# Moving the GpSimd sums and splits of the second MLP layer to VectorE in a one-core decoder trunk

## The chip, the core and the metric

The kernel runs on one core of one Trainium2 chip, in one launch. A core has five engines that each work through a queue of their own in order and wait for one another by semaphores: TensorE (PE in the profile; its weight loads are listed as PEld), VectorE (DVE), ScalarE (ACT), GpSimd (POOL) and SyncE (SP), which here only starts transfers. Transfers run on 16 shared DMA engines. The metric is device time in microseconds (us) of the whole launch; lower is better. Three runs of the kernel before took 2007.76, 2008.43 and 2013.69 us, median 2008.43.

## The reference

With DEPTH = 1 only the first layer runs: a Conformer convolution module and a squared-ReLU MLP, each behind an RMS norm and added to the residual.

```
h = rms_norm(x, mix_norm)                         # x: 1 x 2048 x 1024, float32
a, g = split(h @ w_in + b_in)                     # 1024 -> 2 x 1024
h = depthwise_causal_conv31(a * sigmoid(g)) + conv_b
x = x + silu(layer_norm(h)) @ w_out + b_out
n = rms_norm(x, mlp_norm)
x = x + square(relu(n @ w1)) @ w2                 # 1024 -> 4096 -> 1024
```

The last line's `@ w2` is the "second layer" here: for each token, 4096 hidden values to 1024 outputs.

## The kernel before, in words

Everything is kept transposed: 128 features on the partitions, 512 tokens (T) along the free axis, so the 2048 tokens are four token blocks. Each float32 operand is split in two parts (a rounded part and the rest), and a product is three matmuls: high by high, high by low, low by high.

Token blocks 0 and 1 go through the MLP directly. Token blocks 2 and 3, the last two, go through both MLP layers by a seven-product scheme for 2 x 2 blocks (Strassen's idea in Winograd's form): of the weight blocks A11, A12, A21, A22 it forms S1 = A21 + A22, S2 = S1 - A11, S3 = A11 - A21, S4 = A12 - S2, and it multiplies seven pairs in place of eight.

The second layer of these two token blocks is the last stage, from about 1607 us to the end. It runs over eight groups g of hidden features and two halves o of the outputs, 16 steps in all; here they are called step 0 to step 15, step = 2g + o. A step does this:

- SyncE loads two raw weight tiles (`raw_wq`, L590, tile `rawq`, 512 KB each): a1 holds A11 and A12, a2 holds A21 and A22. There are four such buffers, so a step's two loads go into the buffers of the step two before, once that step has done with them.
- `blocks` (L837) forms the sums: S1 at L842, S2 at L843, S3 in place of A21 at L847, S4 in place of A12 at L849. Then `w_split` (L582 to L586) splits each of the seven blocks: ScalarE casts the high part (L584), and the engine that is handed over subtracts it for the low part (L585). The tile is `wq`; six of them exist, so a split waits until TensorE has done the product six before.
- TensorE does the products in the order P1 (A11), P2 (A12), P6 (S2), P5 (S1), P7 (S3), P3 (S4), P4 (A22), each as two tiles of six matmuls (L609), 84 matmuls in a step. P1, P6, P7 and P4 add up in the same PSUM tiles `px`; after P7 VectorE adds `px` and `p` (L872, "px add" below), and P4 can't write `px` before that read is over.
- The four output pairs leave as adding DMAs (L883, `accum_op=ALU.add`, 512 KB each) that GpSimd issues.
- Every two steps the 14 hidden tiles of a later group are loaded (L598, tile `ld`) and split by ScalarE and VectorE (L92, L93), most of them during an odd step, the last during step 11.

In step 0 VectorE forms S1 and S2, in steps 1 to 15 GpSimd does; the split of A22 is GpSimd's in all 16. A scheduler orders each engine's instructions by the order of the program and its own forecast of when data arrive, so an instruction of a later step can stand in a queue ahead of one of an earlier step.

Of the kernel before, what the change touches and what calls it, by code (L numbers as in the profile page):

```python
# [59 lines left out]
def conformer_mlp(ctx: ExitStack, tc, xT, w_in, w_out, w1, w2, vecs, conv_w, outT):  # L60
    nc = tc.nc
# [371 lines left out]
    def mlp_down(g, blocks, hid, x2, eng=nc.vector):  # L433
        for m in range(KD):
            if m % 2 == 0:
                w = load_w2(g, m, eng)
            for i, b in enumerate(blocks):
                ps = bank()
                mm(ps, lambda k, a: w(m % 2, k, a), hid[i])
                nc.vector.tensor_add(x2[i][m], x2[i][m], ps)  # L440
                if g == NG - 1:
                    nc.sync.dma_start(outT[m * P : (m + 1) * P, b * T : (b + 1) * T], x2[i][m])

    def mlp(g, blocks, x2, xs, eng=nc.vector):
        mlp_down(g, blocks, mlp_up(g, xs, eng), x2, eng)
# [112 lines left out]
    def mid_tile(name):  # L558
        return mid.tile([P, T], F32, name=name, tag="m", bufs=6)
# [22 lines left out]
    def w_split(src, eng):  # L582
        hl = wts.tile([P, 2, T], F32R, name="wq", tag="wq", bufs=N_WQ)
        nc.scalar.copy(hl[:, 0, :], src)  # L584
        eng.tensor_sub(hl[:, 1, :], src, hl[:, 0, :].bitcast(F32))  # L585
        return hl  # L586

    def raw_wq(src):
        t = top.tile([P, 2 * T], F32, name="rawq", tag="rawq", bufs=4)
        nc.sync.dma_start(t if src.shape == t.shape else t.rearrange("p (s q c) -> p s q c", s=2, q=2), src)  # L590
        return t
# [245 lines left out]
    def blocks(g, o):  # L837
        a1, a2 = [raw_wq(w2[g, o][:, 2 * i : 2 * i + 2]) for i in range(2)]
        a11, a12, a21, a22 = a1[:, :T], a1[:, T:], a2[:, :T], a2[:, T:]
        s1, s2 = mid_tile("s1"), mid_tile("s2")  # L840
        eng = nc.gpsimd if g or o else nc.vector
        eng.tensor_add(s1, a21, a22)  # L842
        eng.tensor_sub(s2, s1, a11)  # L843
        out = {"A11": w_split(a11, nc.vector), "A12": w_split(a12, nc.vector)}
        out["S2"] = w_split(s2, nc.vector)
        out["S1"] = w_split(s1, nc.vector)
        nc.vector.tensor_sub(a21, a11, a21)  # L847
        out["S3"] = w_split(a21, nc.vector)
        nc.vector.tensor_sub(a12, a12, s2)  # L849
        out["S4"] = w_split(a12, nc.vector)  # L850
        out["A22"] = w_split(a22, nc.gpsimd)
        return out

    def both(tiles, name, hs, w, first=True):
# [97 lines left out]
```

## Time and profile before

| what | value |
|---|---|
| median of three runs | 2008.43 us |
| the profiled execution, its own time | 2008.22 us |
| its span, first to last instruction | 2006.5 us |
| TensorE busy | 1894.8 us, 94% of the span |
| VectorE busy | 1605.4 us, 80% |
| ScalarE busy | 826.8 us, 41% |
| GpSimd busy | 649.6 us, 32% |
| mean granted TensorE clock | 0.981 of full |

The shares are means over stages that differ. In the last fifth of the span, where the change lies, TensorE is busy some eight tenths of the time and its granted clock dips, while VectorE is at five to six tenths. So the page has to be read by stage: which engine waits, for whom, and what ended that wait last.

### The profile page before, as it was taken

The page shows a single profiled execution, that of the slowest core. Times are in us where ns is not written, and L with a number is a line of the kernel's source. Part 1 is how long each engine was busy: PE and PEld are TensorE (multiplying, and loading weights), DVE is VectorE, ACT ScalarE, POOL GpSimd, SP SyncE. Part 2 cuts the span into 40 slices and gives each one's busy share as a digit, 9 for nine tenths or more (in the row PEclk, how much of TensorE's full clock was granted, in tenths as well). Part 3 has the DMA queues.
Part 4 walks back from the last instruction along what each step waited for, and adds up shares of the span by engine and source line. Part 5 has one row for each costly group of instructions (what it writes and reads, how often), then busy time and mean ns, then how long its engine had stood idle before and what let it go on. Part 6 is the DMA issues. An engine that isn't in the chain of part 4 may idle for free.

```text
span 2006.5 us, 23614 instructions
## 1 busy us (share of the span) xinstructions
PE 1894.8 (94%) x8192; PEld 1546.0 (77%) x8192; DVE 1605.4 (80%) x2318; ACT 826.8 (41%) x1336; POOL 649.6 (32%) x433
## 2 busy tenths in 40 slices
PE   7999999999899999999999989999999978888887
PEld 6888888888778778788888768878888766666675
DVE  7999999999999999799999735695886675565553
ACT  5323225243353333433231524464545655454542
POOL 2256322644445530000000004304665343333333
PEclk9999999999999999999999999999999998999999
DMA  5123222422224333642121458656765687787876
GB/s 197 64 85 116 91 76 73 144 97 98 85 82 144 106 111 111 219 144 98 62 69 65 161 194 292 233 189 225 239 222 187 212 226 199 195 205 199 201 147 182
DMA packets 141623, 303.15 MB, mean 151 GB/s; under 512 B 13632, under 2 KB 40384, under 8 KB 141504
## 3 DMA queue, kind: packets, MB, share of 16 engines
q1 hardware_dynamic: 133440, 272.28, 40.6%
q0 software_dynamic: 8064, 29.36, 8.3%
q8 instruction: 64, 1.05, 0.2%
q14 instruction: 55, 0.45, 0.1%
HBM read 210.12 MB, written 91.47 MB: 150 GB/s over the span
## 4 chain that ended last, share of the span: by engine, by line
PE 37%; issue 9%; DVE 5%; DMA 5%; POOL 3%; ACT 2%; SPq 0%; DVEq 0%; POOLq 0%; ACTq 0%
PE ps L163 16%; PE px L609 12%; PE pz L609 4%; PE py L609 3%; PE px L163 2%; DVE wq L585 1%; POOL x L883 1%; DVE act L93 1%; DMA s<-conv 1%; DMA rawq<-in_w_out 1%; POOL s L842 1%; DMA ld<-hT 1%; DVE p L872 1%; DMA c<-x 1%; ACT act L92 1%
## 5 line engine op out<-in xcount | busy, mean ns | idle before, releaser
L163 PE MATMUL ps<-act,w 128*128 128x512 f32 x2880 | 665.5, 391 | 10.9 <-ACT w L92 8.5
L163 PEld LDWEIGHTS ps<-act,w 128*128 128x128 f32 x2880 | 541.3, 188 | 126.9 <-ACT w L92 8.5
L163 PE MATMUL ps<-hid,w 128*128 128x512 f32 x1920 | 446.2, 392 | 6.1 <-DVE hid L93 5.9
L609 PE MATMUL px<-act,wq 128*128 128x512 f32 x1536 | 386.1, 405 | 61.3 <-DVE p L872 47.7
L163 PEld LDWEIGHTS ps<-hid,w 128*128 128x128 f32 x1920 | 360.5, 189 | 86.8 <-DVE hid L93 8.6
L609 PEld LDWEIGHTS px<-act,wq 128*128 128x128 f32 x1536 | 299.5, 196 | 134.6 <-DVE p L872 53.6
L352 DVE SCALAR_TENSOR_TENSOR cacc<-hc,cw,cacc 128x512 f32<-128x512 f32 x464 | 324.7, 749 | 1.4
L352 DVE SCALAR_TENSOR_TENSOR cacc<-h,cw,cacc 128x512 f32<-128x512 f32 x464 | 316.7, 746 | 0.0
L93 POOL TENSOR_TENSOR w<-raw,w 128x1024 fp32r<-128x1024 f32 x90 | 217.0, 2411 | 288.5 <-ACT w L92 282.7
L92 ACT CAST w<-raw 128x1024 fp32r<-128x1024 f32 (+1 forms) x150 | 155.1, 1035 | 291.0 <-PE ps L163 286.5
L609 PE MATMUL pz<-act,wq 128*128 128x512 f32 x768 | 186.4, 392 | 4.5 <-ACT p L828 2.6
L585 DVE TENSOR_TENSOR wq<-rawq,wq 128x512 fp32r<-128x512 f32 x128 | 123.2, 969 | 68.5 <-ACT wq L584 68.5
L609 PEld LDWEIGHTS pz<-act,wq 128*128 128x128 f32 x768 | 144.9, 189 | 35.5 <-ACT p L828 3.0
L584 ACT CAST wq<-rawq 128x512 fp32r<-128x512 f32 x192 | 117.9, 620 | 124.1 <-DMA rawq<-in_w_out 38.7
L585 POOL TENSOR_TENSOR wq<-rawq,wq 128x512 fp32r<-128x512 f32 x64 | 92.4, 1444 | 236.2 <-ACT wq L584 164.9
L440 DVE TENSOR_TENSOR h<-h,ps 128x512 f32<-128x512 f32 x128 | 86.9, 683 | 31.4 <-PE ps L163 29.7
L427 ACT ACTIVATE relu<-ps 128x512 f32<-128x512 f32 x64 | 38.2, 597 | 161.4 <-PE ps L163 161.3
L93 DVE TENSOR_TENSOR act<-ld,act 128x512 fp32r<-128x512 f32 x112 | 82.6, 756 | 22.7 <-ACT act L92 22.1
L609 PE MATMUL py<-act,wq 128*128 128x512 f32 x384 | 94.6, 395 | 2.9 <-DVE cc L697 2.9
L163 PE MATMUL px<-act,wq 128*128 128x512 f32 x384 | 89.9, 395 | 7.7 <-ACT act L92 7.1
L215 POOL TENSOR_TENSOR acc<-acc,hc 128x512 f32<-128x512 f32 x12 | 14.0, 1163 | 252.1 <-DVE hc L352 201.9
L92 ACT CAST act<-ld 128x512 fp32r<-128x512 f32 x112 | 69.0, 620 | 61.3 <-DMA ld<-hB 27.8
(135 smaller groups left out, 1861.4 us busy)
## 6 DMA issues: line engine op xcount, KB each, us to landing
raw<-in_w SPq DMA_DIRECT2D x104, 512.0 KB, 3.6
rawq<-in_w SPq DMA_DIRECT2D x76, 512.0 KB, 4.9
xt<-in_xT SPq DMA_DIRECT2D x64, 256.0 KB, 3.7
ld<-hT SPq DMA_DIRECT2D x64, 256.0 KB, 5.5
raw<-in_w_in SPq DMA_DIRECT2D x30, 512.0 KB, 3.2
x<-p POOLq DMA_DIRECT2D x28, 512.0 KB, 7.6
hB<-cc SPq DMA_DIRECT2D x48, 256.0 KB, 2.8
ld<-hB SPq DMA_DIRECT2D x48, 256.0 KB, 6.2
```

The lines of the kernel that those rows point to most:

```text
L92: nc.scalar.copy(hl[:, 0, :], src)
L93: eng.tensor_sub(hl[:, 1, :], src, hl[:, 0, :].bitcast(F32))
L163: nc.tensor.matmul(ps, lhsT=w(k, a), rhs=x[:, b, :], start=k == 0 and i == 0, stop=k == len(xs) - 1 and i == 2,)
L352: nc.vector.scalar_tensor_tensor(out, h[:, k : k + T], cw[:, j, k : k + 1], acc, ALU.mult, ALU.add)
L427: nc.scalar.activation(r, ps, AF.Relu)
L440: nc.vector.tensor_add(x2[i][m], x2[i][m], ps)
L584: nc.scalar.copy(hl[:, 0, :], src)
L585: eng.tensor_sub(hl[:, 1, :], src, hl[:, 0, :].bitcast(F32))
L609: nc.tensor.matmul(ps, lhsT=hl[:, a, off + k * P : off + (k + 1) * P], rhs=x[:, b, :], start=first and k == 0 and i == 0, stop=k == n - 1 ...
L842: eng.tensor_add(s1, a21, a22)
L872: nc.vector.tensor_add(c[:, i, :], ps, t[:, i, :])
L883: nc.gpsimd.dma_start(at, c, accum_op=ALU.add)
```

## The change

GpSimd loses three instructions per step: S1, S2 and the low part of A22. VectorE gets them. In the program's text the two sums also move behind the splits of A11 and A12, and since L841 goes, every later line number is smaller by one in the kernel after (L872 becomes L871, L883 becomes L882).

```
-        eng = nc.gpsimd if g or o else nc.vector
-        eng.tensor_add(s1, a21, a22)
-        eng.tensor_sub(s2, s1, a11)
         out = {"A11": w_split(a11, nc.vector), "A12": w_split(a12, nc.vector)}
+        nc.vector.tensor_add(s1, a21, a22)
+        nc.vector.tensor_sub(s2, s1, a11)
         out["S2"] = w_split(s2, nc.vector)
         out["S1"] = w_split(s1, nc.vector)
         nc.vector.tensor_sub(a21, a11, a21)
         out["S3"] = w_split(a21, nc.vector)
         nc.vector.tensor_sub(a12, a12, s2)
         out["S4"] = w_split(a12, nc.vector)
-        out["A22"] = w_split(a22, nc.gpsimd)
+        out["A22"] = w_split(a22, nc.vector)
```

The queues of TensorE keep their order. VectorE's order changes in the second layer only. First place: VectorE in step 4 (even), from the adds of P2 (`p1_13801`) to the px adds (`p5_13846`). `rawq_13965` is a1 of step 5, `rawq_14108` and `rawq_14110` are a1 and a2 of step 6, `s2_13970` is S2 of step 5. Before:

```order
L872 TENSOR_TENSOR p1_13801<-py_13786,p1_13801 128x512
L585 TENSOR_TENSOR wq_13973<-rawq_13965,wq_13973 128x512
L847 TENSOR_TENSOR rawq_14110<-rawq_14108,rawq_14110 128x512
L585 TENSOR_TENSOR wq_13976<-rawq_13965,wq_13976 128x512
L849 TENSOR_TENSOR rawq_13965<-rawq_13965,s2_13970 128x512
L585 TENSOR_TENSOR wq_13979<-s2_13970,wq_13979 128x512
L872 TENSOR_TENSOR p5_13846<-px_13783,p5_13846 128x512
```

The same place in the kernel after, from the split of A22 of step 4 (`wq_13780`) on:

```order
L585 TENSOR_TENSOR wq_13780<-rawq_13754,wq_13780 128x512
L871 TENSOR_TENSOR p1_13801<-py_13785,p1_13801 128x512
L871 TENSOR_TENSOR p1_13801<-py_13786,p1_13801 128x512
L585 TENSOR_TENSOR wq_13971<-rawq_13965,wq_13971 128x512
L842 TENSOR_TENSOR s1_14112<-rawq_14110 128x512
L843 TENSOR_TENSOR s2_14113<-s1_14112,rawq_14108 128x512
L846 TENSOR_TENSOR rawq_14110<-rawq_14108,rawq_14110 128x512
L585 TENSOR_TENSOR wq_13974<-rawq_13965,wq_13974 128x512
L848 TENSOR_TENSOR rawq_13965<-rawq_13965,s2_13970 128x512
L585 TENSOR_TENSOR wq_13979<-s2_13970,wq_13979 128x512
L871 TENSOR_TENSOR p5_13846<-px_13783,p5_13846 128x512
```

In both, an instruction on step 6's weights stands ahead of step 4's px add: before it is L847, which waits for GpSimd's S1 of step 6; after it is S1 itself, then S2, then the same subtraction.

Second place: VectorE in step 3 (odd), from the split of A11 of step 4 to the px add (`p5_13703`), with the splits of hidden tiles (L93) between. `rawq_13967` is a2 of step 5. Before:

```order
L585 TENSOR_TENSOR wq_13760<-rawq_13752,wq_13760 128x512
L93 TENSOR_TENSOR act_13917<-ld_13915,act_13917 128x512
L93 TENSOR_TENSOR act_13922<-ld_13920,act_13922 128x512
L847 TENSOR_TENSOR rawq_13967<-rawq_13965,rawq_13967 128x512
L585 TENSOR_TENSOR wq_13763<-rawq_13752,wq_13763 128x512
L93 TENSOR_TENSOR act_13927<-ld_13925,act_13927 128x512
L849 TENSOR_TENSOR rawq_13752<-rawq_13752,s2_13757 128x512
L93 TENSOR_TENSOR act_13932<-ld_13930,act_13932 128x512
L585 TENSOR_TENSOR wq_13766<-s2_13757,wq_13766 128x512
L872 TENSOR_TENSOR p5_13703<-px_13640,p5_13703 128x512
```

After:

```order
L93 TENSOR_TENSOR act_13917<-ld_13915,act_13917 128x512
L842 TENSOR_TENSOR s1_13969<-rawq_13967 128x512
L93 TENSOR_TENSOR act_13922<-ld_13920,act_13922 128x512
L843 TENSOR_TENSOR s2_13970<-s1_13969,rawq_13965 128x512
L585 TENSOR_TENSOR wq_13761<-rawq_13752,wq_13761 128x512
L93 TENSOR_TENSOR act_13927<-ld_13925,act_13927 128x512
L848 TENSOR_TENSOR rawq_13752<-rawq_13752,s2_13757 128x512
L93 TENSOR_TENSOR act_13932<-ld_13930,act_13932 128x512
L585 TENSOR_TENSOR wq_13766<-s2_13757,wq_13766 128x512
L871 TENSOR_TENSOR p5_13703<-px_13640,p5_13703 128x512
```

S1 and S2 of step 5 stand where L847 stood; that subtraction (now L846) comes 20 instructions later, behind the px adds.

Third place: GpSimd in steps 3 and 4. Before, the adding DMAs stand between sums and split:

```order
L842 TENSOR_TENSOR s1_13969<-rawq_13967 128x512
L843 TENSOR_TENSOR s2_13970<-s1_13969,rawq_13965 128x512
L883 DMA x2_1_3_9335<-p5_13703 128x1024
L883 DMA x2_1_2_9334<-u2_13688 128x1024
L883 DMA x2_0_3_9331<-c_13748 128x1024
L585 TENSOR_TENSOR wq_13780<-rawq_13754,wq_13780 128x512
```

After, from the DMA ahead of these on:

```order
L882 DMA x2_0_2_9330<-p1_13658 128x1024
L882 DMA x2_1_3_9335<-p5_13703 128x1024
L882 DMA x2_1_2_9334<-u2_13688 128x1024
L882 DMA x2_0_3_9331<-c_13748 128x1024
L882 DMA x2_0_0_9328<-p1_13801 128x1024
```

Up to step 13, only the issuing of the adding DMAs is left on GpSimd in this layer.

## Rows read from the trace of the kernel before

**Rows 1.** Two stretches: start:end us, busy PE, PEld, DVE, ACT, POOL, clock, DMA, GB/s

```profile
1500.00:1600.00 100.00, 98.11 (x429) 80.77 (x428) 68.05 (x81) 60.00 (x105) 49.85 (x35) 0.99 0.56 194
1750.00:1800.00 50.00, 41.83 (x176) 33.55 (x175) 29.40 (x44) 26.25 (x47) 17.14 (x16) 0.93 0.82 205
```

**Rows 2.** Who waited for whom, 1645 to 2007: us in total, times, longest

```profile
DVE rawq L847 <- POOL s L842: 92.8, 13, 11.7
POOL s L842 <- DMA rawq<-in_w: 80.6, 13, 9.9
...
PE px L609 <- DVE p L872: 47.4, 13, 7.2
```

**Rows 3.** Timeline of TensorE, P4 with the next P1: start, us, [idle before]

```profile
1654.65 7.35 PE L609 MATMUL px<-act,wq 128*128 128x512 f32 x24 [2.96 <-DVE p L872]
...
1681.88 7.88 PE L609 MATMUL px<-act,wq 128*128 128x512 f32 x24 [6.29 <-DVE p L872]
...
1704.60 5.74 PE L609 MATMUL px<-act,wq 128*128 128x512 f32 x24 [1.24 <-DVE p L872]
...
1782.30 7.16 PE L609 MATMUL px<-act,wq 128*128 128x512 f32 x24 [6.29 <-DVE p L872]
...
1881.97 8.46 PE L609 MATMUL px<-act,wq 128*128 128x512 f32 x24 [6.02 <-DVE p L872]
...
1904.19 5.73 PE L609 MATMUL px<-act,wq 128*128 128x512 f32 x24 [0.16 <-DVE p L872]
...
1926.89 5.75 PE L609 MATMUL px<-act,wq 128*128 128x512 f32 x24 [3.37 <-DVE p L872]
```

**Rows 4.** Timeline of step 2 (even), landing of step 4's weights to px add

```profile
1676.25 1.25 POOL L842 TENSOR_TENSOR s<-rawq 128x512 f32<-128x512 f32 x1 [9.56 <-DMA rawq<-in_w]
1677.54 0.69 DVE L847 TENSOR_TENSOR rawq<-rawq 128x512 f32<-128x512 f32 x1 [11.38 <-POOL s L842]
1677.58 1.77 POOL L843 TENSOR_TENSOR s<-s,rawq 128x512 f32<-128x512 f32 x1
1678.15 1.75 DVE L585 TENSOR_TENSOR wq<-rawq,wq 128x512 fp32r<-128x512 f32 x1
1679.93 0.69 DVE L849 TENSOR_TENSOR rawq<-rawq,s 128x512 f32<-128x512 f32 x1
1680.54 0.69 DVE L585 TENSOR_TENSOR wq<-s,wq 128x512 fp32r<-128x512 f32 x1
1681.14 1.28 DVE L872 TENSOR_TENSOR p<-px,p 128x512 f32<-128x512 f32 x2
```

**Rows 5.** Timeline of step 3 (odd), landing of step 5's weights to px add

```profile
1697.82 1.29 POOL L842 TENSOR_TENSOR s<-rawq 128x512 f32<-128x512 f32 x1 [2.86 <-DMA rawq<-in_w]
...
1699.75 1.78 DVE L585 TENSOR_TENSOR wq<-rawq,wq 128x512 fp32r<-128x512 f32 x1
...
1703.87 0.67 DVE L872 TENSOR_TENSOR p<-px,p 128x512 f32<-128x512 f32 x1
```

**Rows 6.** Timeline of step 2: A22's split, and step 4's two weight loads

```profile
1661.83 3.94 SPq L590 DMA_DIRECT2D rawq<-in_w  x2
...
1663.40 0.62 ACT L584 CAST wq<-rawq 128x512 fp32r<-128x512 f32 x1
...
1664.11 1.30 POOL L585 TENSOR_TENSOR wq<-rawq,wq 128x512 fp32r<-128x512 f32 x1 [3.08 <-ACT wq L584]
```

**Rows 7.** Stretches of 3 us in steps 2 and 3, columns as in rows 1

```profile
1664.00:1667.00 3.00, 3.00 (x15) 2.49 (x14) 1.68 (x3) 1.72 (x4) 2.18 (x2) 1.00 1.05 263
...
1676.00:1679.00 3.00, 0.00 (x0) 0.00 (x0) 1.46 (x2) 0.25 (x1) 2.67 (x2) 1.00 0.01 4
...
1682.00:1685.00 3.00, 3.00 (x7) 2.37 (x8) 2.82 (x5) 0.15 (x1) 1.35 (x2) 0.50 0.31 29
...
1700.00:1703.00 3.00, 3.00 (x15) 2.44 (x13) 3.00 (x4) 1.16 (x3) 0.98 (x1) 1.00 0.71 210
```

**Rows 8.** Instructions on `rawq` from 1600 us: ns min/median/max, first and last start

```profile
L585 DVE TENSOR_TENSOR wq<-rawq,wq x62: 672/684/1790, 1613.1 to 1974.4; 128x512 fp32r<-128x512 f32 x62
```

## The prediction, made before the changed kernel ran

> **What bounds the kernel now.** I read the page by slices first, then the last stage by stretches. In a stretch before the second layer TensorE is busy 98 of 100 us, in one inside it 42 of 50, with the clock at 0.93 and VectorE at 29 of 50 [rows 1]. So TensorE waits there, and not because VectorE is full.
>
> The waits of that stage say for whom. The largest wait of TensorE is for the px add: 47.4 us in 13 waits. VectorE itself waits 92.8 us in 13 times at L847 for GpSimd's S1, and GpSimd waits 80.6 us in 13 times for the raw weights [rows 2]. These are one chain: a weight tile of a later step lands, GpSimd adds S1, VectorE goes on with what stands ahead of the px add in its queue, then the px add lets P4 start.
>
> The timeline of step 2 shows it link by link [rows 4]. The weights land at 1676.25; S1 takes 1.25; L847 starts at 1677.54; the split of A12 takes 1.75 beside GpSimd's S2; L849 and the split of S2 follow; the px add starts at 1681.14. That is 4.89 us from landing to px add, and P4 starts when the first of its two halves is done, at 1681.88, after 6.29 us of idle TensorE [rows 3]. In step 3 the same chain, with hidden splits between, takes from 1697.82 to 1703.87, 6.05 us [rows 5], and P4 waits 1.24 us. After the long wait 24 matmuls take 7.88 us where they take 5.74 after a short one [rows 3]; the granted clock in that stretch is 0.50, the lower of the two levels [rows 7].
>
> The loop closes through the DMA engines. They are full while weights, hidden tiles and results move (1.05 in rows 7) and empty at 1676 to 1679, when VectorE works off the chain (0.01). So the time of two steps, 1654.65 to 1704.60 or 50 us [rows 3], is one stretch of transfers, a chain, another stretch, another chain. Shorten the chain and the next transfers start earlier.
>
> **The change part by part.** It removes 15 S1, 15 S2 and 16 low parts of A22 from GpSimd (1.25, 1.77 and 1.30 us in step 2) [rows 4, 6] and adds them to VectorE. One there takes 0.69 us alone (median 684 ns) [rows 8], and instructions in a row start 0.61 us apart (1679.93, 1680.54, 1681.14) [rows 4]. VectorE's load grows by 46 x 0.61 = 28 us in a stage where it is idle four tenths of the time [rows 1].
>
> Even chain. Six VectorE instructions now stand from landing to px add (S1, S2, the subtraction, split of A12, L848, split of S2): 6 x 0.61 = 3.7, and 0.1 each for the two that wait for the result just ahead of them (a full 0.69 in place of 0.61), 3.9 us. Before it was 4.89. Gain 1.0 in each of steps 2, 4, 6, 8, 10, 12 and 13: **7.0**. Ends: without any such wait 3.7, a gain of 1.2; if each of the six waits 0.2 for the one ahead, 6 x 0.81 = 4.9 and the gain is 0. I take the end near the 0.61 of the rows.
>
> Odd chain. Eight instructions from landing to px add, 8 x 0.61 = 4.9, against 6.05: gain 1.15. It counts in steps 3, 5, 7, 9: **4.6**. In step 11 P4 waited 0.16 us only [rows 3], which is what I count: **0.2**. That P4 waits only 1.24 in step 3 doesn't cap it, since an earlier px add also starts the results and the next loads earlier.
>
> Step 1. In the new order step 3's sums stand behind step 1's px add, so that wait goes as a whole. Its P4 waited 2.96 us [rows 3]. Late next are the hidden splits ahead of the px add, for which I keep 1.2 of it. Gain **1.75**.
>
> A22's low part. In step 2 ScalarE's cast ends at 1663.40 + 0.62 = 1664.02; GpSimd's split runs to 1665.41, and the second weight load goes out behind it (the two issues of 1661.83 last 3.94 us) [rows 6]. VectorE would be done at 1664.02 + 0.04 + 0.69 = 1664.75, 0.66 earlier. Where the DMA engines are full, an earlier issue brings less; I take 0.2 for each of ten steps, and 0.6 in steps 12 and 13, where the hidden loads are over: 10 x 0.2 + 2 x 0.6 = **3.2**. Ends: 0, and 12 x 0.66 = 7.9. In the queue it stands ahead of the P2 adds, which come 0.6 later; they fill tiles that TensorE wants again a step later, so nobody waits.
>
> What moves. L846 stands ahead of the split of S4 in even steps, so the first of two weight loads can go out 0.6 later; the second one, which lands last, doesn't depend on it. The adding DMAs on GpSimd lose the sums ahead of them, but they wait for VectorE's adds, not for GpSimd. The port: the split beside GpSimd's S2 takes 1.75 and alone 0.69, 1.06 more; this is inside the chains above (4.89 and 6.05) and isn't counted twice.
>
> The Trainium skill, page "SBUF — State Buffer", section "SBUF: two separate sides", says that VectorE with two SBUF inputs and a GpSimd instruction that reads SBUF lock each other out for a whole instruction. Taken to its end, each of the 46 could have blocked VectorE for its length, 15 x (1.25 + 1.77 + 1.30) = 65 us, and the time would be 1943. The trace shows one blocked split per chain, 13 x 1.06 = 14 us; the row decides.
>
> Sum: 7.0 + 4.6 + 0.2 + 1.75 + 3.2 = 16.75. The profiled execution took 2008.2 (span 2006.5 and 1.7 around it), 0.2 below the median of 2008.43. **2008.2 - 16.75 = 1991.5 us.**
>
> **The rivals.**
>
> *The DMA queue takes it back.* If the transfers, not the chain, set when weights land, an earlier px add only finds them still busy. For it: 1.05 at 1664 to 1667, and still 0.71 at 1700 to 1703, when the odd chain runs [rows 7]. Against it: 0.01 during the even chain. Then the gains of the odd chains and of A22 go, except in steps 1, 12 and 13: 7.0 + 1.75 + 1.2 = 9.95, **1998.2**. [...]
>
> *TensorE keeps its clock.* Seven of the 13 waits were followed by 24 matmuls in 7.16 to 8.46 us, the others by about 5.74 [rows 3]. The excess over 5.74 of the seven adds up to 13.9 us. A wait of 3.37 us was followed by 5.75 [rows 3], so waits that fall by 1 us or more might spare it. Then 1991.5 - 13.9 = **1977.6**. Against it: after 2.96 us it was slow [rows 3].
>
> *No change.* The weights land later by what the chains gain, since results and loads compete in another order: **2008**, within 2003 to 2014. This is also where it ends if the even chain keeps its 4.89 because each instruction waits for the one ahead.
>
> *VectorE becomes the bound, slower.* The three new instructions of a step stand ahead of the px add in a queue that works in order. If the weights have landed by the time VectorE gets to S1, nothing hides them: 15 x 3 x 0.61 = 27.5, less 13 x 1.06 = 13.8 for the lock, +13.7: **2021.9**. It decides from the point where VectorE has no idle time ahead of S1. Against it: 92.8 us of idle time in just that place, 11.38 in step 2 [rows 2, 4].
>
> **How the numbers follow.** Forecast 0.52 (1986 to 1998), DMA queue 0.17 (to 2003), clock kept 0.13, no change 0.12, slower 0.06. A measurement of this kernel can tell about 0.3%, 6 us: faster is below 2002.4. That is the forecast, the clock, and nearly all of the queue case: 0.80; same 0.14; slower 0.06. The range 1976 to 2003 leaves out no change and slower and a little of the clock case, 0.2.
>
> **What would show it.** Right: the wait of GpSimd for weights turns into one of VectorE at L842; from there to the px add 3.9 us in even steps and 4.9 in odd ones; no split of VectorE near 1.75 in the layer; P4's waits some 5 us in even steps and near none in odd ones; two steps in about 47.5 us; second loads out some 0.6 earlier behind the cast of A22. Wrong: the landing comes later against the px add before it (queue); P4's 24 matmuls all near 5.74 (clock); VectorE without idle time ahead of L842 (slower). The sum is wrong if the stage up to 1600 us changes, since nothing is moved there.

## The result and the profile after

The changed kernel took 1989.21 us (median of 4 runs, 1986.6 to 1991.83) against 2009.41 for the kernel before beside it: ratio 0.9896, 95% interval 0.9875 to 0.9917, or 17 to 25 us less. The forecast was 1991.5, within 1976 to 2003. The profiled execution, the fastest of the four, took 1986.6 us with a span of 1984.8, which is 21.7 below the span before; the medians lie 20.2 apart.

First the two stretches of [rows 1] in the trace after, with the same columns:

```profile
1500.00:1600.00 100.00, 98.10 (x427) 80.72 (x426) 66.51 (x80) 60.05 (x105) 49.68 (x34) 0.98 0.57 195
1750.00:1800.00 50.00, 44.35 (x185) 35.83 (x186) 32.53 (x53) 27.39 (x51) 7.84 (x9) 0.93 0.88 219
```

Ahead of the second layer nothing changed (TensorE 98.10 of 100 us, 98.11 before). Inside it TensorE works 44.35 of 50 us where it worked 41.83, GpSimd less than half as long, and the DMA engines are fuller (0.88 for 0.82) because the same bytes pass in less time. The waits that answer to [rows 2]:

```profile
DVE s L842 <- DMA rawq<-in_w: 67.6, 12, 9.9
...
PE px L609 <- DVE p L871: 30.2, 7, 6.3
```

GpSimd's wait for weights has become VectorE's wait at L842, as the forecast said, and P4's waits for the px add fell from 13 (47.4 us) to 7 (30.2 us). Next TensorE's timeline with P4, from step 1 on, to lay beside [rows 3]; the columns are start, length, and the idle time ahead with what ended it:

```profile
1646.76 5.60 PE L609 MATMUL px<-act,wq 128*128 128x512 f32 x24
...
1672.14 8.49 PE L609 MATMUL px<-act,wq 128*128 128x512 f32 x24 [4.27 <-DVE p L871]
...
1694.07 5.60 PE L609 MATMUL px<-act,wq 128*128 128x512 f32 x24
...
1719.18 7.25 PE L609 MATMUL px<-act,wq 128*128 128x512 f32 x24 [5.09 <-DVE p L871]
...
1766.38 7.53 PE L609 MATMUL px<-act,wq 128*128 128x512 f32 x24 [5.14 <-DVE p L871]
...
1905.36 7.35 PE L609 MATMUL px<-act,wq 128*128 128x512 f32 x24 [3.63 <-DVE p L871]
...
1926.14 5.60 PE L609 MATMUL px<-act,wq 128*128 128x512 f32 x24
```

Even steps still wait some 5 us and still run the next 24 matmuls slowly; odd steps hardly wait. Two steps last 47.2 us (1719.18 to 1766.38) where the same two lasted 49.3 (1733.00 to 1782.30). The chain behind the landing of weights, in step 4 (VectorE's timeline, every row of it):

```profile
1714.57 0.69 DVE L842 TENSOR_TENSOR s<-rawq 128x512 f32<-128x512 f32 x1 [8.67 <-DMA rawq<-in_w]
1715.30 0.69 DVE L843 TENSOR_TENSOR s<-s,rawq 128x512 f32<-128x512 f32 x1
1715.91 0.68 DVE L846 TENSOR_TENSOR rawq<-rawq 128x512 f32<-128x512 f32 x1
1716.51 0.69 DVE L585 TENSOR_TENSOR wq<-rawq,wq 128x512 fp32r<-128x512 f32 x1
1717.23 0.69 DVE L848 TENSOR_TENSOR rawq<-rawq,s 128x512 f32<-128x512 f32 x1
1717.84 0.69 DVE L585 TENSOR_TENSOR wq<-s,wq 128x512 fp32r<-128x512 f32 x1
1718.44 1.28 DVE L871 TENSOR_TENSOR p<-px,p 128x512 f32<-128x512 f32 x2
```

From landing to px add it is 3.87 us, against 4.89 in [rows 4]. The starts are 0.60 or 0.61 apart, and 0.72 or 0.73 at two places, behind L842 and ahead of L848. Up to step 13 no split of the layer is near 1.75 any more; the two that are left, 1.81 and 1.58 at 1940.63 and 1947.08, lie beside GpSimd's additions of the last two steps (L879). The odd chain of step 3, which answers to [rows 5]:

```profile
1688.21 0.69 DVE L842 TENSOR_TENSOR s<-rawq 128x512 f32<-128x512 f32 x1 [2.36 <-DMA rawq<-in_w]
...
1693.04 0.68 DVE L871 TENSOR_TENSOR p<-px,p 128x512 f32<-128x512 f32 x1
```

That is 4.83 us for 6.05. And the second weight load of a step, which goes out behind A22's split, here in step 4 ([rows 6] have it in step 2):

```profile
1701.56 2.90 SPq L590 DMA_DIRECT2D rawq<-in_w  x2
...
1702.76 0.62 ACT L584 CAST wq<-rawq 128x512 fp32r<-128x512 f32 x1
...
1703.41 0.69 DVE L585 TENSOR_TENSOR wq<-rawq,wq 128x512 fp32r<-128x512 f32 x1 [0.31 <-ACT wq L584]
```

The issue is over at 1704.46, 1.08 after the end of the cast at 1703.38. In [rows 6] it was 1665.77 after 1664.02, 1.75; so 0.67 earlier.

**What had not been forecast stands in steps 0 and 1.** In the trace before, the timelines of VectorE, GpSimd, ScalarE and TensorE in that stretch read:

```profile
1616.59 6.24 DVE L93 TENSOR_TENSOR act<-ld,act 128x512 fp32r<-128x512 f32 x5
...
1628.52 2.21 DVE L847 TENSOR_TENSOR rawq<-rawq 128x512 f32<-128x512 f32 x1
...
1617.75 1.62 POOL L842 TENSOR_TENSOR s<-rawq 128x512 f32<-128x512 f32 x1
1619.45 1.63 POOL L843 TENSOR_TENSOR s<-s,rawq 128x512 f32<-128x512 f32 x1
...
1628.61 1.56 POOL L843 TENSOR_TENSOR s<-s,rawq 128x512 f32<-128x512 f32 x1
...
1630.89 0.62 ACT L584 CAST wq<-rawq 128x512 fp32r<-128x512 f32 x1 [2.98 <-DVE rawq L847]
1631.42 1.06 ACT L876 COPY c<-px 128x512 f32<-128x512 f32 x2
...
1632.05 2.93 PE L609 MATMUL px<-act,wq 128*128 128x512 f32 x6 [2.94 <-ACT c L876]
1634.77 3.13 PE L609 MATMUL py<-act,wq 128*128 128x512 f32 x12
```

Five splits of hidden tiles take 6.24 us beside S1 and S2 of step 1, and L847 takes 2.21 beside S2 of step 2. VectorE has no idle time there. ScalarE's cast behind L847 comes late, the copy of `c` stands behind that cast, and P4 of step 0 waits 2.94 us for it. The same places after (VectorE and TensorE):

```profile
1615.88 3.09 DVE L93 TENSOR_TENSOR act<-ld,act 128x512 fp32r<-128x512 f32 x5
...
1624.59 5.60 PE L609 MATMUL px<-act,wq 128*128 128x512 f32 x24
1630.03 2.88 PE L609 MATMUL py<-act,wq 128*128 128x512 f32 x12
```

The five take 3.09, and P4 of step 0 runs through. At P2 of step 1 (1630.03 for 1634.77) the changed kernel is already 4.7 us ahead, before any of the chains that the forecast counted.

### The profile page after: what moved, and what is told of

Its sections match the earlier page's. It is cut to its first block, busy times and chain, and to the rows that moved or that the text cites. A ratio compares the mean times of both kernels' runs of the same rounds, so it can differ in the third digit from the quotient of the medians.

```text
span 1984.8 us, 23561 instructions
## 1 busy us (share of the span) xinstructions
PE 1889.5 (95%) x8192; PEld 1544.2 (78%) x8192; DVE 1609.1 (81%) x2364; ACT 824.7 (42%) x1336; POOL 585.2 (29%) x387
## 4 chain that ended last, share of the span: by engine, by line
PE 39%; DMA 10%; DVE 5%; issue 3%; ACT 2%; POOL 0%; SPq 0%; DVEq 0%; ACTq 0%; POOLq 0%
PE ps L163 16%; PE px L609 11%; PE pz L609 5%; PE px L163 4%; DMA rawq<-in_w 4%; PE py L609 2%; DMA ld<-hB 2%; DMA ld<-hT 2%; DVE wq L585 1%; DVE act L93 1%; DMA c<-x 1%; ACT act L92 1%; ACT wq L584 0%; DMA x<-c 0%; DMA c<-conv 0%
## 5 line engine op out<-in xcount | busy, mean ns | idle before, releaser
L609 PE MATMUL px<-act,wq 128*128 128x512 f32 x1536 | 381.3, 402 | 44.1 <-DVE p L871 30.2
L609 PEld LDWEIGHTS px<-act,wq 128*128 128x128 f32 x1536 | 297.0, 195 | 114.5 <-DVE p L871 33.8
L93 POOL TENSOR_TENSOR w<-raw,w 128x1024 fp32r<-128x1024 f32 x90 | 218.1, 2424 | 287.2 <-ACT w L92 281.3
L585 DVE TENSOR_TENSOR wq<-rawq,wq 128x512 fp32r<-128x512 f32 x144 | 116.3, 815 | 74.4 <-ACT wq L584 74.2
L585 POOL TENSOR_TENSOR wq<-rawq,wq 128x512 fp32r<-128x512 f32 x48 | 71.5, 1491 | 192.4 <-ACT wq L584 176.5
L93 DVE TENSOR_TENSOR act<-ld,act 128x512 fp32r<-128x512 f32 x112 | 79.2, 726 | 23.5 <-ACT act L92 23.0
L163 PEld LDWEIGHTS px<-act,wq 128*128 128x128 f32 x384 | 73.4, 192 | 24.8 <-ACT act L92 8.4
L882 POOL DMA_DIRECT2D x<-p x28 | 24.4, 872 | 230.3 <-DVE p L871 221.8
```

What stands on the lines that cost most here:

```text
L163: nc.tensor.matmul(ps, lhsT=w(k, a), rhs=x[:, b, :], start=k == 0 and i == 0, stop=k == len(xs) - 1 and i == 2,)
L609: nc.tensor.matmul(ps, lhsT=hl[:, a, off + k * P : off + (k + 1) * P], rhs=x[:, b, :], start=first and k == 0 and i == 0, stop=k == n - 1 ...
L882: nc.gpsimd.dma_start(at, c, accum_op=ALU.add)
```

## The experiments

Each is given as a ratio to the kernel before on the same chip with its 95% interval; "us" beside it is its distance from 1, or from the ratio that it is compared with, times 2010. Theory at the start: a wait for weights stands ahead of the px add in VectorE's queue, and the change shortens what lies between the two, by S1's longer time on GpSimd and by VectorE instructions that GpSimd holds up.

**Which part brings it.** Four kernels with one part each. Only the sums, A22 back on GpSimd:

```
-        out["A22"] = w_split(a22, nc.vector)
+        out["A22"] = w_split(a22, nc.gpsimd)
```

> The kernel after, with the low part of A22 left on GpSimd: only S1 and S2 move to VectorE. Theory (the chain behind the landing weights, and the pairs of GpSimd and VectorE instructions that slow each other in steps 0 and 1): the sums carry all but the 3.2 us that the prediction gave to A22, so 3 us above the kernel after, near 1992 to 1993, with landing to px add near 3.6 us in even steps and the first matmul of P2 in step 1 some 4.5 us earlier than before. Rival (the earlier issue of the second weight load is what counts, because the loop runs through the DMA engines): most of the gain goes, 2000 or more.

Measured 1993.58, ratio 0.9921 (0.9907 to 0.9934): 16 us gained. The chain of step 4 is 3.87 long, not near 3.6. Then the kernel before with only A22 moved:

```
-        out["A22"] = w_split(a22, nc.gpsimd)
+        out["A22"] = w_split(a22, nc.vector)
```

> The kernel before, with only the low part of A22 on VectorE; S1 and S2 stay on GpSimd where they stood. Theory: 2 to 4 us below before (the prediction's term is 3.2), near 2005, with the landing to px add still 4.9 in step 2 and splits near 1.75 still there. Rival (the second load's issue counts): 10 us or more below before, under 1999.

Measured 2007.65, ratio 0.9984 (0.9970 to 0.9998): 3 us, with chains of 4.89 and 6.04. The sums carry the gain, and the two parts add up to the whole (16 + 3, against 21). Then the order of the source alone:

```
-        eng.tensor_add(s1, a21, a22)
-        eng.tensor_sub(s2, s1, a11)
         out = {"A11": w_split(a11, nc.vector), "A12": w_split(a12, nc.vector)}
+        eng.tensor_add(s1, a21, a22)
+        eng.tensor_sub(s2, s1, a11)
```

> The sums stand behind the splits of A11 and A12 in the program, as in the kernel after, but on GpSimd; A22 on GpSimd too. So the order of the source alone is changed. Theory: the engine counts and not the place in the source, so within 3 us of before, 2005 to 2011. Rival (the place in the source makes the gain): within 5 us of after, 1986 to 1994.

Measured 2010.45, ratio 1.0000 (0.9988 to 1.0013). The place in the source does nothing that shows beyond 2.6 us. Last, the kernel before with S1 and S2 of two steps on VectorE:

```
-        eng = nc.gpsimd if g or o else nc.vector
+        eng = nc.gpsimd if 2 * g + o > 2 else nc.vector
```

> The kernel before, with S1 and S2 of steps 1 and 2 alone on VectorE. Theory: the two traces differ by 4.7 us already at P2 of step 1 and 7.9 us at P4 of step 1, because the sums of steps 1 and 2 on GpSimd lengthened VectorE's work where VectorE had no idle time; so these two steps alone bring 5 to 8 us, 2000 to 2003, with P2 of step 1 near 1630 and no wait of P4 in step 0. Rival (the prediction's terms as they stand, a gain of about 1 in step 2 and some of 1.75 in step 1): 1 to 3 us, 2005 to 2007.

Measured 2006.08, ratio 0.9979 (0.9968 to 0.9991), 4 us (2 to 6): between the 5 to 8 of the theory and the rival's 1 to 3, and the interval reaches into both. In its trace P6 of step 0 starts at 1613.61 and P2 of step 1 at 1632.65, 19.0 us later; before it is 23.3 (1611.48 to 1634.77), after 18.8 (1611.25 to 1630.03). That alone doesn't show that these sums cost 4.3 us there: with A22 alone moved and the sums still on GpSimd it is 18.6 (1614.27 to 1632.83). P6 itself waits 2.2 to 5.1 us in the profiles of all these kernels, whatever they change (2.19 before, 2.90 after, 4.35 here, 5.14 with A22 alone), and a long wait there hides what comes behind; it was not followed up. A longer stretch takes that wait in: from the 24 matmuls that end with P1 of step 0 to P4 of step 1 the kernels with the sums on GpSimd take 53.8 (before), 55.2 (order of the source) and 52.8 us (A22 alone), this one 50.2, and the kernel after 46.3. So moving these two steps' sums brings 3 to 5 us there, one execution each.

**Length of the chain or something else.** The kernel after, with two dummy subtractions on GpSimd at the place of S1 and S2; their result is not read:

```
+        if g or o:
+            for _ in range(2):
+                nc.gpsimd.tensor_sub(dum, a22, a22)
         out["S2"] = w_split(s2, nc.vector)
...
+    dum = top.tile([P, T], F32, name="dum", tag="dum", bufs=1)
```

> The kernel after, with two subtractions on GpSimd in every step but the first, at the place of S1 and S2 (each reads A22 twice and writes a tile that nobody reads); all real work is as in the kernel after. Theory (a good part of what was removed is VectorE instructions lengthened beside GpSimd's): splits or sums near 1.3 to 1.8 us come back beside each dummy, and the time rises by 8 to 17 us, to 1997 to 2006. Rival (only the place of S1 in the chain and its own 1.25 us counted): within 3 us of after.

Measured 2009.76, ratio 0.9991 (0.9976 to 1.0005). The whole gain is gone, a little more than the theory's 8 to 17. The chain in step 2 (its VectorE and GpSimd timelines; L851 and L849 are S4 and S3), the next adding DMA, and in the last line the two dummies of step 3's weights, at a time when VectorE does nothing:

```profile
1673.44 0.69 DVE L842 TENSOR_TENSOR s<-rawq 128x512 f32<-128x512 f32 x1 [7.40 <-DMA rawq<-in_w]
1674.05 1.53 DVE L585 TENSOR_TENSOR wq<-rawq,wq 128x512 fp32r<-128x512 f32 x1
1675.50 1.52 DVE L843 TENSOR_TENSOR s<-s,rawq 128x512 f32<-128x512 f32 x1
1676.95 0.68 DVE L851 TENSOR_TENSOR rawq<-rawq,s 128x512 f32<-128x512 f32 x1
...
1678.75 1.28 DVE L876 TENSOR_TENSOR p<-px,p 128x512 f32<-128x512 f32 x2
...
1673.56 2.92 POOL L846 TENSOR_TENSOR dum<-rawq 128x512 f32<-128x512 f32 x2 [6.96 <-DMA rawq<-in_w]
1680.33 0.88 POOL L887 DMA_DIRECT2D x<-p  x1 [3.85 <-DVE p L876]
...
1646.39 2.16 POOL L846 TENSOR_TENSOR dum<-rawq 128x512 f32<-128x512 f32 x2 [5.13 <-DMA rawq<-in_w]
```

The chain has the same six VectorE instructions as in the kernel after, in another order. Each dummy holds up one of them: 1.53 and 1.52 in place of 0.69. The dummies are held up too: the pair takes 2.92 us here and 2.16 beside an idle VectorE. They don't delay the adding DMA behind them in GpSimd's queue, which waits 3.85 us more for the px add. From landing to px add it is 5.31 here and 5.43 in the other even steps, 6.52 in odd ones. Against the kernel after (3.87 and 4.83) that is 1.69 more in step 2 and in five odd chains and 1.56 in six even ones, 19.5 us of chain. The ratios of the two kernels lie 0.0095 apart, 19 us, but the time doesn't follow the chain one to one. Of the 21.7 us between the two spans 15.4 arise where these chains lie, from P4 of step 1 to P4 of step 13 (294.77 and 279.38), and 4.8 ahead of them, from P1 of step 0 to P4 of step 1 (51.06 and 46.31). Nor did the kernel before have as much of this: it had one split held up in a chain, at 1.75, where the dummies hold up two instructions. The run shows that hold-ups have this price; that it ends at the time of the kernel before is in part chance. The Trainium skill, page "SBUF — State Buffer", section "SBUF: two separate sides", says of VectorE with two SBUF inputs and a GpSimd instruction that reads SBUF that the one that starts first has the shared port for its whole instruction and blocks the other. These rows agree: in the chain one VectorE instruction is held up for each of GpSimd's. The forecast bounded this rule at its far end (65 us); one held-up instruction per dummy is where it stands.

Holding up VectorE is not all that S1 on GpSimd does: it also waits for weights ahead of adding DMAs in GpSimd's queue. A much smaller dummy tells the two apart:

```
+        if g or o:
+            nc.gpsimd.tensor_sub(dum, a22[:, :1], a22[:, :1])
         out["S2"] = w_split(s2, nc.vector)
...
+    dum = top.tile([P, 1], F32, name="dum", tag="dum", bufs=1)
```

> The kernel after, with one 128x1 subtraction on GpSimd in every step but the first, which reads A22 and whose result nobody reads. It stands where S1 stood in GpSimd's queue, ahead of the adding DMA of the px add, and waits for the same weights, but is too small to hold VectorE up. Theory (the two full dummies of the earlier run brought the whole gain back by blocking VectorE's instructions): within 4 us of after, 1986 to 1994. Rival (it is GpSimd's wait for weights ahead of the adding DMAs that cost the time): 2000 to 2010.

Measured 1990.31, ratio 0.9886 (0.9869 to 0.9904), the same as after. Its step 4 (GpSimd's and VectorE's timelines), and in the last line a dummy beside an idle VectorE:

```profile
1714.41 0.63 POOL L845 TENSOR_TENSOR dum<-rawq 128x1 f32<-128x1 f32 x1 [8.86 <-DMA rawq<-in_w]
...
1714.29 0.69 DVE L842 TENSOR_TENSOR s<-rawq 128x512 f32<-128x512 f32 x1 [9.30 <-DMA rawq<-in_w]
1715.02 0.69 DVE L843 TENSOR_TENSOR s<-s,rawq 128x512 f32<-128x512 f32 x1
...
1640.07 0.19 POOL L845 TENSOR_TENSOR dum<-rawq 128x1 f32<-128x1 f32 x1 [4.62 <-DMA rawq<-in_w]
```

Here it is the dummy that is held up: it starts 0.12 behind L842, ends 0.06 behind it and takes 0.63 where it takes 0.19 beside an idle VectorE. VectorE's instructions keep their 0.69. GpSimd's wait for weights costs nothing that shows in this kernel; its full-size instructions cost 19 to 21 us.

**Why landing to px add counts at all.** Two kernels attack the wait itself. In the first, VectorE writes a 128x1 tile with the value 1 behind the px add of step n, and S1 and the splits of A11 and A12 of step n+2 are multiplied by it, so that they can't stand ahead of that px add:

```
             out(1, 1, px, p5)
...
+                nc.vector.tensor_scalar(toks[2 * g + o], p5[:, 1, 0:1], 0.0, 1.0, ALU.mult, ALU.add)
...
-        nc.vector.tensor_add(s1, a21, a22)
...
+            nc.vector.scalar_tensor_tensor(s1, a21, tok, a22, ALU.mult, ALU.add)
...
```

> The kernel after, with S1 and the splits of A11 and A12 of step n+2 made to depend on a 128x1 value that VectorE writes right behind the px add of step n (they are multiplied by it, and it is 1). In the kernel after, S1 of step 4 stands ahead of the px add of step 2 in VectorE's queue, and so on; here it stands behind it. Nothing else is left out; a step gets one 128x1 instruction more. Theory (the wait of P4 is an instruction that waits for weights standing ahead of the px add, and the weights themselves are early enough): the 30 us of waits in 7 P4s nearly vanish and the clock stays up behind them; two steps fall from 47.2 to 44 or 45 us; 1965 to 1975. Rival (the DMA engines set the pace, so the wait only moves to the next place that needs the weights, P6 or P1 two steps on): 1984 to 1992.

Measured 1956.80, ratio 0.9723 (0.9701 to 0.9746): 35 us below after by the ratios and below the range of the theory. In its trace, P4 of steps 2 to 4 in TensorE's timeline and the px add and the next S1 in VectorE's, step 4:

```profile
1672.72 5.60 PE L612 MATMUL px<-act,wq 128*128 128x512 f32 x24
...
1691.76 5.60 PE L612 MATMUL px<-act,wq 128*128 128x512 f32 x24
...
1711.17 5.60 PE L612 MATMUL px<-act,wq 128*128 128x512 f32 x24
...
1708.65 0.69 DVE L879 TENSOR_TENSOR p<-px,p 128x512 f32<-128x512 f32 x1 [0.29 <-PE px L612]
...
1712.36 0.75 DVE L849 SCALAR_TENSOR_TENSOR s<-rawq,tok 128x512 f32<-128x512 f32 x1 [1.64 <-DMA rawq<-in_w]
```

And a longer stretch of the layer, with the columns of [rows 1], first here and then in the kernel after:

```profile
1640.00:1900.00 260.00, 243.17 (x1046) 195.93 (x1045) 190.10 (x311) 146.58 (x264) 42.87 (x50) 0.99 0.94 231
...
1640.00:1900.00 260.00, 225.55 (x935) 181.59 (x934) 163.09 (x264) 136.13 (x246) 38.18 (x44) 0.94 0.85 212
```

The px add no longer waits for weights, P4 follows without idle time (0.2 us in later odd steps), its 24 matmuls take 5.60 to 5.74, and two steps take 38.5 us (1672.72 to 1711.17; later pairs 40 to 45). Between 1640 and 1900 TensorE is busy 243.17 us at a clock of 0.99, in the kernel after 225.55 us at 0.94. So the wait was one of place: these weights are wanted two steps later. The second kernel leaves the place and loads earlier:

```
-        t = top.tile([P, 2 * T], F32, name="rawq", tag="rawq", bufs=4)
+        t = top.tile([P, 2 * T], F32, name="rawq", tag="rawq", bufs=5)
```

> The kernel after with five buffers for raw weight tiles in place of four, so that one weight load of a step can go out a step earlier. The order of some VectorE instructions ahead of 1600 us changes with it, so only the stretch behind counts. Theory (px adds wait behind the landing of weights that were issued late): landings come earlier against the px add, the even waits of P4 shrink from 5 us, and the second layer is 5 to 15 us shorter, 1975 to 1985. Rival (the DMA engines have no room, the landing stays where it is): 1986 to 1992.

Measured 1977.85, ratio 0.9827 (0.9807 to 0.9847), 14 us below after. The time is the theory's, the mechanism isn't shown. The profiled execution is the slowest of the five (1983.93), its span only 2.7 below that of the kernel after. In it the landing does come earlier behind the even px adds, 14.7 us for 16.6, but the odd chains got longer, 7.23 for 4.83, and P4's waits came to 25.3 us in 12. Where the 14 us come from was not settled. Both together:

> The kernel with the 128x1 value and the change, with five buffers for raw weight tiles in place of four. Theory (with the px adds ahead of the waits for weights, the landing of weights no longer sets anything): within 4 us of the same kernel with four buffers, 1953 to 1961. Rival (the two gains add, since earlier loads also spare waits for hidden tiles): 1940 to 1948.

Measured 1946.81, ratio 0.9670 (0.9656 to 0.9685). The theory fails and the rival holds: the buffer brings 11 us here too. TensorE is busy 250.88 of 260 us from 1640 to 1900. This is the fastest version found; it beats both kernels.

**Is the move worth less once the px add is ahead?** The kernel before (sums and A22 on GpSimd), with the 128x1 value in S3 (L847) and in the splits of A11 and A12:

```
-        nc.vector.tensor_sub(a21, a11, a21)
...
+            nc.vector.scalar_tensor_tensor(a21, a11, tok, a21, ALU.mult, ALU.subtract)
```

> The kernel before (S1, S2 and the low part of A22 on GpSimd) with the 128x1 value of the earlier experiment: the first difference and the splits of A11 and A12 of step n+2 are multiplied by it on VectorE, so that VectorE's first instruction for step n+2 stands behind the px add of step n. Theory (GpSimd's sums cost time only where VectorE's px add stands behind them): without that place the wait of P4 goes here too, and what is left of GpSimd's cost, some locked instructions, is partly hidden: 1957 to 1972, so the move of the change would be worth 0 to 15 us here. Rival (the move to VectorE is worth its 20 us wherever the px add stands): 1975 to 1980.

Measured 1981.39, ratio 0.9850 (0.9833 to 0.9867). The theory fails: P4's waits went here too (one of 0.88 us is left), but the move is worth 25 us on top of that (0.9850 against 0.9723), no less than in the kernel as it was. The waits of TensorE have another name. From its waits, 1640 to 1930:

```profile
ACT act L92 <- DMA ld<-hT: 52.2, 17, 7.1
...
PE pz L612 <- ACT p L831: 26.4, 12, 4.0
```

With the value and the sums on VectorE these two are 37.4 and 11.7 us, and the granted clock between 1640 and 1900 is 0.99, here 0.93. Read together, ScalarE waits for hidden tiles ahead of its copy of `pz`, and TensorE waits for the copy; what makes the hidden tiles later here, and what the lower clock adds, was not shown. To divide the 25 us, the two dummies were put into the kernel with the 128x1 value, the small one and then the two full ones (the edits as above):

> The kernel with the 128x1 value (sums on VectorE, px add ahead of S1) and the same 128x1 subtraction on GpSimd, ahead of the adding DMA of the px add. With the sums on GpSimd this kernel took 1981.4, with them on VectorE 1956.8. Theory now: with the px add ahead, GpSimd's wait for weights delays the adding DMAs by 3 to 6 us, and that is most of the 24.6 between the two: 1972 to 1981. Rival (blocked VectorE instructions and GpSimd's own durations): 1955 to 1960.

Measured 1963.65, ratio 0.9751 (0.9729 to 0.9773): 6 us above the same kernel without it, with intervals that overlap. So the wait in GpSimd's queue is not most of the 25, as the theory had it; the rival, at most 1960, misses by less.

> The kernel with the 128x1 value, with the two full dummy subtractions of the earlier run on GpSimd. It has the wait in GpSimd's queue and the blocked VectorE instructions. Theory: 1976 to 1984, at most 6 us above the kernel with the small dummy, because a blocked instruction stands behind the px add here. Rival (blocked instructions cost here as they did in the kernel after, 20 us): 15 us or more above the kernel with the small dummy.

Measured 1974.65, ratio 0.9812 (0.9790 to 0.9835): 12 us above the small dummy, between the two expectations. The full dummies cost about half of the 25 us here as well. The 8 us that are left, between this kernel and the one with the sums on GpSimd, would be A22 and the longer GpSimd sums; that was not separated.

## Why the prediction was right

**Even chain, 7.0.** Right, mechanism and size: 3.9 forecast, 3.87 measured in all but step 2 (3.61, where the split of A12 stands between S1 and S2 and every start is 0.60 or 0.61 behind the one ahead). The 0.1 allowed for each of two instructions that wait for the one ahead shows as 0.12 in the rows of step 4. Seven chains shortened by 7.5.

**Odd chain, 4.6, and step 11, 0.2.** Right: 4.9 forecast, 4.83 measured. Four chains are 4.9 shorter. Step 11's is 1.23 shorter where 0.2 was counted: the landing behind it moved away by 1.5 (17.77 us behind the px add before, 19.27 after), but the next came closer by as much (16.93 and 15.46).

**A22, 3.2.** Right within what can be told: the load goes out 0.67 earlier (0.66 forecast), and A22 alone measured 3 us (0.4 to 6). In this pair of traces the twelve distances from a px add to the next landing, where an earlier load would show, fell by 1.9 us together.

These three can be checked as one: from P4 of step 1 to P4 of step 13 the kernel before takes 294.12 us (1654.65 to 1948.77), the kernel after 279.38 (1646.76 to 1926.14). The last P4 before:

```profile
1948.77 7.34 PE L609 MATMUL px<-act,wq 128*128 128x512 f32 x24 [2.53 <-DVE p L872]
```

That is 14.7 gained where 15.0 were forecast. So close a match is luck in part. The same stretch takes 300.3 us in the kernel with only the order of the source changed and 283.5 in the one with the small dummy, so the gain is some 11 to 21 us by which execution is taken. And the 14.7 hold 1.75 that the forecast did not count (the 24 matmuls at P4 of step 1 take 5.60 for 7.35, since the wait ahead of them is gone) and lack 1.60 (those at P4 of step 12 take 7.35 for 5.75).

**Step 1, 1.75: the term that was mis-sized.** From the 24 matmuls that end with P1 of step 0 (1600.83 and 1600.45) to P4 of step 1 the gain is 7.5 us; with 55.2 us (order) and 47.5 (small dummy) for 53.8 and 46.3 it would be 6 to 9. 3.2 of it lie behind P2 of step 1: the wait of 2.96 went as a whole, and nothing of the 1.2 that the forecast kept back came late. The other 4.4 lie ahead of it. The forecast counted held-up splits only inside the chains ("this is inside the chains above (4.89 and 6.05) and isn't counted twice"); in steps 0 and 1 they stood where VectorE had no idle time, and everything behind moved. Some of the 7.5 is A22's, to which the forecast gave nothing in these two steps: with A22 left on GpSimd the stretch takes 50.3, in one execution. At the other end 0.9 was lost behind P4 of step 13, and 0.4 had been gained ahead of step 0: 14.7 + 7.5 + 0.4 - 0.9 = 21.7, the difference of the spans. In this pair the total lies 5 us beyond the sum of 16.75, and this one term, which was 5.8 too small, is why; by the medians it is 3.5 beyond, with 17 to 25 as the interval.

**The rivals.** *DMA queue:* fell. Landing kept its distance from the px add ahead of it: over the five even steps 2 to 10 a mean of 16.61 us before and 16.55 after, and over the odd ones 3 to 9 22.37 and 21.94. *Clock:* fell for this change. Six waits of 3.63 to 6.29 us were still followed by 24 matmuls of 7.25 to 8.49. Steps 1 and 13, which no longer wait, were spared, and step 12 (3.63 for 3.37) became slow, so the excess over 5.74 fell from 13.9 us to 11.8 only. That it can be had, the kernel with the 128x1 value shows. *VectorE full:* fell, 67.6 us of idle time are left ahead of L842. *No change:* fell, the even chains came to 3.87 and not 4.89, and the landing didn't take it back.

## What to carry to other kernels

When GpSimd and VectorE work on SBUF side by side, read the lengths of VectorE's instructions beside GpSimd's, and charge each lengthened one in every place where VectorE's queue has no slack, not only in the chain under study. An engine's queue is in order: a wait ahead of an instruction that TensorE wants should be looked for first, and its place may be worth more than its length (35 us here against 21). A theory on why a change works is tested best by putting the suspected cost back alone, as the dummies did.

## What the runs showed that had not been expected

Hold-ups go both ways. VectorE's 128x512 instruction takes 1.53 us in place of 0.69 when GpSimd's began ahead of it; GpSimd's 128x1 subtraction takes 0.63 in place of 0.19 when VectorE's began ahead, and leaves VectorE's as they are. One more 512 KB buffer for weights was worth 11 to 14 us with either order of the px add, though only one of the two kernels waited at the px add.
